# S5's inputs as products of x times the norm's weight, with the tokens' roots at the eviction, and S5's parameters on GpSimd

## The chip, the cores and the metric

One core of a Trainium2 chip runs the whole program in one launch. The metric is the device time in microseconds (us) of one execution. The engines are named as in the profile: PE (TensorE's matmuls; PEld its weight loads), DVE (VectorE), ACT (ScalarE), POOL (GpSimd) and SP (SyncE, which here only issues DMAs).

## What is computed

One layer of a decoder trunk over x (1024 tokens of 1024 channels, float32). Only the beginning matters here:

```python
h = x * rsqrt(mean(x * x, -1) + 1e-6) * norm_mix_pre
proj = h @ w_in          # columns: RWKV-7 parts | S5's input u (512) | two gates (2048)
# S5, 32 groups of 16 channels, 64 complex states each:
lam = a_re + 1j * a_im;  dt = exp(log_step);  a_bar = exp(lam * dt)
b_bar = ((a_bar - 1) / lam) * (b_re + 1j * b_im)
states = scan(a_bar, b_bar @ u);  y = Re(c @ states) + d * u
```

After it follow S5's GELU and gate, RWKV-7's recurrence, the merge of both branches, an output projection, and a gated MLP with a convolution, each with its norm.

## The kernel before

Everything is stored with channels on the 128 partitions and tokens along the free axis, in two halves of 512 tokens (`th` 0 and 1); x is 8 tiles of 128x512 per half. A float32 product is made of three matmuls on halves of the operands: `hi` is the operand rounded to fp32r (a cast on ACT), `lo` the rest (a subtraction on DVE or POOL), and hi*hi + hi*lo + lo*hi is accumulated (L169, L170, L171). So each 128x128 block of weights costs three matmuls of 128x512 per half.

The front of the program is this, in the order of PE's queue, which is that of the code (`manual_schedule` for PE; on the other engines the framework orders instructions by readiness and by the priorities HPN > HPW > HP2 > HP):

- Norm of half 0 (`norm`, L949 to L967): load x, square on ACT (L952), add pairs on DVE (L953), sum over channels by tiny matmuls against ones (`sumsq`, L242), the reciprocal root by bit trick and three Newton steps on DVE (`rstd` L262, `rsqrt` L131 to L136), its broadcast to all partitions by four transposes (`spread`, L268), a copy on ACT (`rbc`, L961). Then x times weight times root on DVE (L964) and its halves `hh` (ACT, L223) and `hl` (DVE or POOL, L224).
- S5's input u (`s5_in`, L1057): four output tiles (columns 14 to 17 of `w_in`), for both halves: 2 x 4 x 8 x 3 = 192 matmuls, in rounds of 12 for each of the 8 x tiles. Each of the four sums is copied out of PSUM by ACT (L1070) and written to DRAM (`US`), from where it comes back rearranged (`u8`).
- Norm of half 1, beside it, through the same steps.
- S5's parameters (`s5_setup`, L303 to L475): about 110 small operations on DVE, nearly all of 128x32, and a few sines on ACT.
- Then `mix_in` (L1034 on): the RWKV columns. Its first tile is column tile 12, which needs the scaled halves hh and hl of the norm. Beside it, S5's tables (`s5_tables`, L486 on) and scan run on DVE, and their small matmuls stand between those of `w_in`.

The parts after that are the same before and after the change.

Of the kernel before, what the change touches and what calls it, by code (L numbers as in the profile page):

```python
# [18 lines left out]
D = 1024  # L19
# [47 lines left out]
class Kern:  # L67
# [204 lines left out]
    def setup(self):  # L272
        nc = self.nc
        self.vecs = self.const.tile([128, NVEC], F32, name="vecs")
        self.csts = self.const.tile([128, NCST], F32, name="csts")
        nc.gpsimd.dma_start(self.csts[:, 0:128], self.a["cst"][:, 0:128])
        nc.gpsimd.dma_start(self.vecs, self.a["vec"])
        nc.gpsimd.dma_start(self.csts[:, 128:NCST], self.a["cst"][:, 128:NCST])
# [6 lines left out]

        o, n = VEC["mu"]
# [15 lines left out]
    def s5_setup(self):  # L302
        nc, V = self.nc, self.nc.vector  # L303
# [3 lines left out]
        with self.tc.tile_pool(name="s5tmp", bufs=1) as pool:  # L307
# [3 lines left out]
            nc.sync.dma_start(ls, a["s5_ls"])  # L311
            nc.sync.dma_start(lr, a["s5_a"][0])
            nc.sync.dma_start(li, a["s5_a"][1])
# [14 lines left out]
            def stt(x, sc, y, o0, o1):  # L328
                z = sm()
                V.scalar_tensor_tensor(z, x, sc, y, o0, o1)  # L330
                return z
# [50 lines left out]
            def sincos(x):  # L382
                x = ts(x, -PI_, PI_, ALU.max, ALU.min)
                si, co, ab = sm(), sm(), sm()
                nc.scalar.activation(si, x, AF.Sin)
# [17 lines left out]
            V.reciprocal(rd, d1)  # L403
# [71 lines left out]
            nc.sync.dma_start(s["d"], a["s5_d"])  # L475
# [460 lines left out]
    def load_x(self, th, pool):  # L936
        xs = []
        for k in range(NK):
            x = pool.tile([128, 512], F32, name=self.nm("x"), tag="x", bufs=16)
            self.nc.sync.dma_start(x, self.a["x"][k * 128:k * 128 + 128, th * 512:th * 512 + 512])  # L940
            xs.append(x)
        return xs

    def norm(self, th, xs, pool):

        nc = self.nc
        ss = self.chk()[:, 0:512]
        yield 0, T_X
        for k in range(0, NK, 2):  # L949
            sq = [pool.tile([128, 512], F32, tag="sq", name=self.nm("sq"), bufs=4) for _ in range(2)]  # L950
            for i in range(2):
                nc.scalar.activation(sq[i], xs[k + i], AF.Square)  # L952
            nc.vector.tensor_tensor(sq[0], sq[0], sq[1], ALU.add)  # L953
            self.sumsq(ss, sq[0], k == 0)
            yield 0.9, 1.0
        bc = self.chk()[:, 0:512]
        y = self.rstd(ss, 1e-6, 1.0 / D)
        yield 0, T_RS
        self.spread(bc, y)
# [97 lines left out]
    def s5_in(self, pool):  # L1057

        w = [self.load_w(self.a["w_in"][14 + b], pool=pool if b > 1 else None) for b in range(4)]
        for th in range(2):  # L1060
# [3 lines left out]
            for k in range(NK):  # L1064
                for b in range(4):
                    yield next(steps[b])
# [879 lines left out]
```

## Time and the profile before

| | us |
|---|---|
| median of 3 runs (lowest, highest) | 1556.08 (1554.93, 1562.61) |
| the profiled execution's own time | 1555.05 |
| its span in the profile | 1553.3 |
| PE busy in the span | 1455.0 |
| first matmul of S5's input | at 26.00 |
| first matmul of column tile 12, right behind S5's input | at 79.55 |

All times in the text are positions in the span or lengths, in us. In the lists of instructions, a row has its start, its length, the engine, the line in the kernel, the operation, output <- inputs, shapes, and in square brackets how long the engine was idle before it and what ended that. A length on DVE or POOL holds the time in which a started instruction could not get at its data; the start to start distance of neighbours shows the pipelined rate.

### The profile page before, as it was taken

To read this page: it belongs to the slowest core of one execution; us is meant where nothing else is said; L and a number is where in the kernel's file an instruction comes from. 1 tells how busy PE (TensorE), PEld (TensorE's weight loads), DVE (VectorE), ACT (ScalarE), POOL (GpSimd) and SP (SyncE) were. 2 spreads that over 40 slices of the span, in tenths; PEclk is the share of its full clock that TensorE was granted. 3 is DMA by queue.
4 is the path that set the end of the run, shared out by engine and by line. 5 is a ranking of instruction groups with operands and counts; after the bars stand their busy time and mean duration, and the time that the engine had idled before them with its cause. 6 is when DMAs were issued, how large, how long until landed. Compare 5 with 4: busy or idle time off the path is not lost. (4 is left out here: it accounts for less than half of the span.)

```text
span 1553.3 us, 24246 instructions
## 1 busy us (share of the span) xinstructions
PE 1455.0 (94%) x9324; PEld 1189.1 (77%) x9324; DVE 1092.0 (70%) x1777; ACT 682.4 (44%) x1061; POOL 135.9 (9%) x161
## 2 busy tenths in 40 slices
PE   5999899899999798999888999999999999999994
PEld 4787788778878586777776888788888887888783
DVE  6798784745326649547786689777777777697676
ACT  5354442433324444436434455444444444443450
POOL 2120000621103410100000000000000000000000
PEclk9999999999999999999998999999999999999997
DMA  6164342633413564524874444222222226934712
GB/s 208 41 202 119 93 126 92 203 116 109 152 48 99 158 193 145 148 70 111 263 232 154 160 146 142 82 87 84 85 88 84 82 69 230 325 129 148 240 60 94
DMA packets 131107, 210.45 MB, mean 135 GB/s; under 512 B 37696, under 2 KB 43840, under 8 KB 130992
## 3 DMA queue, kind: packets, MB, share of 16 engines
q1 hardware_dynamic: 124208, 188.32, 38.6%
q0 software_dynamic: 5632, 18.49, 3.7%
q10 hardware_dynamic: 1152, 2.10, 0.4%
q8 instruction: 73, 1.20, 0.3%
q14 instruction: 42, 0.34, 0.1%
HBM read 153.28 MB, written 53.48 MB: 133 GB/s over the span
## 5 line engine op out<-in xcount | busy, mean ns | idle before, releaser
L169 PE MATMUL gm<-hh,wh 128*128 128x512 f32 x688 | 283.0, 411 | 14.8 <-DVE hl L1115 8.9
L170 PE MATMUL gm<-hl,wh 128*128 128x512 f32 x688 | 271.4, 394 | 0.4 <-DVE hl L224 0.4
L171 PE MATMUL gm<-hh,wl 128*128 128x512 f32 x656 | 258.1, 394 | 0.0
L154 DVE TENSOR_TENSOR wl<-wf,wh 128x512 fp32r<-128x512 f32 x175 | 124.2, 711 | 116.0 <-ACT wh L153 106.9
L153 ACT CAST wh<-wf 128x512 fp32r<-128x512 f32 x179 | 110.5, 618 | 207.1 <-PE gm L170 118.5
L169 PEld LDWEIGHTS gm<-hh,wh 128*128 128x128 f32 x688 | 131.1, 190 | 50.1 <-DVE hl L1115 10.9
L170 PEld LDWEIGHTS gm<-hl,wh 128*128 128x128 f32 x688 | 131.0, 190 | 26.1 <-issue 1.0
L171 PEld LDWEIGHTS gm<-hh,wl 128*128 128x128 f32 x656 | 124.3, 190 | 27.3
L1554 PE MATMUL d<-xl,wh 128*128 128x512 f32 x308 | 121.7, 395 | 6.9 <-DVE xl L224 6.9
L1553 PE MATMUL d<-xh,wh 128*128 128x512 f32 x308 | 121.3, 394 | 2.1 <-ACT xh L223 2.1
L1555 PE MATMUL d<-xh,wl 128*128 128x512 f32 x308 | 120.9, 393 | 0.0
L1379 PE MATMUL rp<-t,h 128*128 128x512 f32 x216 | 84.4, 391 | 1.8 <-ACT p L1393 1.8
L1381 PE MATMUL rp<-t,l 128*128 128x512 f32 x216 | 84.1, 390 | 0.5 <-DVE l L224 0.5
L1380 PE MATMUL rp<-t,h 128*128 128x512 f32 x216 | 84.1, 389 | 0.0
L1554 PEld LDWEIGHTS d<-xl,wh 128*128 128x128 f32 x308 | 58.6, 190 | 20.7 <-DVE xl L224 8.6
L1553 PEld LDWEIGHTS d<-xh,wh 128*128 128x128 f32 x308 | 58.4, 190 | 14.7 <-ACT xh L223 2.5
L1555 PEld LDWEIGHTS d<-xh,wl 128*128 128x128 f32 x308 | 58.7, 191 | 12.3
L223 ACT CAST h<-r 128x1024 fp32r<-128x1024 f32 x34 | 35.8, 1054 | 61.1 <-PE rp L1380 29.6
L224 DVE TENSOR_TENSOR l<-r,h 128x1024 fp32r<-128x1024 f32 x34 | 41.6, 1225 | 29.2 <-ACT h L223 27.7
L1400 DVE SCALAR_TENSOR_TENSOR y<-zv,vecs,y 128x1023 f32<-128x1023 f32 (+1 forms) x36 | 46.1, 1281 | 8.6 <-ACT y L1398 8.6
L1379 PEld LDWEIGHTS rp<-t,h 128*128 128x128 f32 x216 | 40.5, 188 | 11.3 <-ACT p L1393 2.7
L1381 PEld LDWEIGHTS rp<-t,l 128*128 128x128 f32 x216 | 40.5, 188 | 9.4 <-DVE l L224 1.0
(451 smaller groups left out, 3244.0 us busy)
## 6 DMA issues: line engine op xcount, KB each, us to landing
r<-in_w_up_dram SPq DMA_DIRECT2D x36, 512.0 KB, 3.6
wf<-in_w_in_dram SPq DMA_DIRECT2D x68, 256.0 KB, 3.1
st<-in_w_down_dram SPq DMA_DIRECT2D x55, 256.0 KB, 4.2
st<-ACT SPq DMA_DIRECT2D x44, 256.0 KB, 4.5
wf<-in_w_up_dram SPq DMA_DIRECT2D x36, 256.0 KB, 2.8
ACT<-y POOLq DMA_DIRECT2D x18, 512.0 KB, 2.9
GT<-ev SPq DMA_DIRECT2D x32, 256.0 KB, 2.4
wf<-in_w_br_dram SPq DMA_DIRECT2D x32, 256.0 KB, 3.4
```

The lines of the kernel that those rows point to most:

```text
L153: nc.scalar.copy(h[:, :n], f[:, :n])
L154: nc.vector.tensor_tensor(l[:, :n], f[:, :n], h[:, :n].bitcast(F32), ALU.subtract)
L169: mm(ps, a, xh[k], start=k == 0, stop=False)
L170: mm(ps, a, xl[k], start=False, stop=False)
L171: mm(ps, b, xh[k], start=False, stop=k == n - 1)
L1379: mm(ps, wh[:, c], xh, start=first and k == 0, stop=False, skip_group_check=True)
L1380: mm(ps, wh[:, c], xl, start=False, stop=False, skip_group_check=True)
L1381: mm(ps, wl[:, c], xh, start=False, stop=k == 3, skip_group_check=True)
L1400: V.scalar_tensor_tensor(y[:, lag:], z[:, 0:1024 - lag], self.vec(nme, i), y[:, lag:], ALU.mult, ALU.add)
L1553: mm(ps, wh[:, c], xh[:, x], start=start, stop=False, skip_group_check=True)
L1554: mm(ps, wh[:, c], xl[:, x], start=False, stop=False, skip_group_check=True)
L1555: mm(ps, wl[:, c], xh[:, x], start=False, stop=stop, skip_group_check=True)
```

## The change

S5's input is no longer made from the finished norm. `start` loads x and the weights first of all, forms x times the norm's weight alone (`gained`: ACT's cast with a scale, DVE's rest with the same scale), multiplies that with the four weight tiles, and multiplies each token's root in when the sums leave PSUM (`evict`, on DVE in place of ACT's copy). The scaled halves that the other columns need (`scaled`) are made afterwards, into the same buffers, when S5's matmuls have read the unscaled ones. The squares are summed on DVE and POOL to one tile per half, so that four tiny matmuls per half are left of 16. The vectors of parameters come on ACT's DMA queue, the large constants on SP's behind x. The first weight tiles land in the `u8` buffers, which are free until then. `s5_setup` runs on POOL (only the reciprocal stays on DVE; a scalar_tensor_tensor becomes two POOL operations), its four small loads are on POOL's queue, and its sines are tied behind ACT's copy of the broadcast root of half 0.

```diff
--- before.py
+++ after.py
@@ -273,9 +273,8 @@
         nc = self.nc
         self.vecs = self.const.tile([128, NVEC], F32, name="vecs")
         self.csts = self.const.tile([128, NCST], F32, name="csts")
+        nc.scalar.dma_start(self.vecs, self.a["vec"])
         nc.gpsimd.dma_start(self.csts[:, 0:128], self.a["cst"][:, 0:128])
-        nc.gpsimd.dma_start(self.vecs, self.a["vec"])
-        nc.gpsimd.dma_start(self.csts[:, 128:NCST], self.a["cst"][:, 128:NCST])
         self.ones1 = self.const.tile([128, 1], F32, name="ones1")
         nc.gpsimd.memset(self.ones1, 1.0)
         self.last = self.const.tile([128, 14], F32, name="last")
@@ -283,6 +282,8 @@
         self.hpi = self.const.tile([128, 1], F32, name="hpi")
         nc.gpsimd.memset(self.hpi, math.pi / 2)

+    def setup_vecs(self):
+        nc = self.nc
         o, n = VEC["mu"]
         self.mu1 = self.const.tile([128, n], F32, name="mu1")
         nc.vector.tensor_scalar(self.mu1, self.vecs[:, o:o + n], -1.0, 1.0, ALU.mult, ALU.add)
@@ -300,7 +301,7 @@


     def s5_setup(self):
-        nc, V = self.nc, self.nc.vector
+        nc, V = self.nc, self.nc.gpsimd
         c = self.s5c
         a = self.a
         self.s5 = s = {}
@@ -308,9 +309,9 @@
             def sm(n=32, dt=F32):
                 return pool.tile([128, n], dt, name=self.nm("sm"))
             lr, li, ls = sm(), sm(), sm()
-            nc.sync.dma_start(ls, a["s5_ls"])
-            nc.sync.dma_start(lr, a["s5_a"][0])
-            nc.sync.dma_start(li, a["s5_a"][1])
+            nc.gpsimd.dma_start(ls, a["s5_ls"])
+            nc.gpsimd.dma_start(lr, a["s5_a"][0])
+            nc.gpsimd.dma_start(li, a["s5_a"][1])

             def ts(x, s1, s2, o0, o1=None, out=None, n=32):
                 y = out if out is not None else sm(n)
@@ -327,7 +328,8 @@

             def stt(x, sc, y, o0, o1):
                 z = sm()
-                V.scalar_tensor_tensor(z, x, sc, y, o0, o1)
+                V.tensor_scalar(z, x, sc, None, o0)
+                V.tensor_tensor(z, z, y, o1)
                 return z

             def rnd(x, sc):
@@ -382,6 +384,7 @@
             def sincos(x):
                 x = ts(x, -PI_, PI_, ALU.max, ALU.min)
                 si, co, ab = sm(), sm(), sm()
+                nc.scalar.copy(si[:, 0:1], self.rbc[:, 0:1])
                 nc.scalar.activation(si, x, AF.Sin)
                 nc.scalar.activation(ab, x, AF.Abs)
                 nc.scalar.activation(co, ab, AF.Sin, bias=self.hpi, scale=-1.0)
@@ -400,7 +403,7 @@
             d2 = tt(li, li, ALU.mult)
             d1 = tt(d1, d2, ALU.add)
             rd = sm()
-            V.reciprocal(rd, d1)
+            nc.vector.reciprocal(rd, d1)
             u1, u2 = tt(nr, lr, ALU.mult), tt(ni, li, ALU.mult)
             qr = tt(tt(u1, u2, ALU.add), rd, ALU.mult)
             u1, u2 = tt(ni, lr, ALU.mult), tt(nr, li, ALU.mult)
@@ -472,7 +475,7 @@
             V.tensor_scalar(q2[64:128], ar[64:128], -1.0, None, ALU.mult)
             s["q1"], s["q2"] = q1, q2
             s["d"] = c.tile([16, 32], F32, name="s5d")
-            nc.sync.dma_start(s["d"], a["s5_d"])
+            nc.gpsimd.dma_start(s["d"], a["s5_d"])


     def s5_load(self, b):
@@ -933,38 +936,121 @@
                 yield from self.mm3_steps(ps, w, 0, [h[0] for h in self.h[th]], [h[1] for h in self.h[th]])
                 use(th, ps)

-    def load_x(self, th, pool):
...
-    def norm(self, th, xs, pool):
...
+    def start(self, pool):
+
+        nc, V, A, G = self.nc, self.nc.vector, self.nc.scalar, self.nc.gpsimd
+        raw = {}
+        xs = [[pool.tile([128, 512], F32, name=self.nm("x"), tag="x", bufs=16) for k in range(NK)] for th in range(2)]
+        w = [([], []) for b in range(4)]
+
+        def load_x(th, k):
+            nc.sync.dma_start(xs[th][k], self.a["x"][k * 128:k * 128 + 128, th * 512:th * 512 + 512])
+
+        def load_w(b, i):
+            if b < 3:
+                f = self.u8[b].rearrange("p g n -> p (g n)")[:, i * 512:i * 512 + 512]
+            else:
+                f = self.wp.tile([128, 512], F32, tag="wf", name=self.nm("wf"), bufs=NWF)
+            raw[b, i] = f
+            nc.sync.dma_start(f, self.a["w_in"][14 + b][:, i * 512:i * 512 + 512])
+
+        def split_w(b, i):
+            own = pool if b > 1 else self.wp
+            h = own.tile([128, 512], F32R, tag="wh", name=self.nm("wh"), bufs=4 if b > 1 else NWH)
+            l = self.lx() if b > 1 else own.tile([128, 512], F32R, tag="wl", name=self.nm("wl"), bufs=NWL)
+            self.split(h, l, raw[b, i])
+            w[b][0].append(h)
+            w[b][1].append(l)
+
+        def gained(th, k):
+            hi, lo = self.pair(th, k)
+            g = self.vec("g_mix_pre", k)
+            A.activation(hi, xs[th][k], AF.Identity, scale=g)
+            V.scalar_tensor_tensor(lo, xs[th][k], g, hi.bitcast(F32), ALU.mult, ALU.subtract)
+            return hi, lo
+
+        def square(th, k):
+            sq = pool.tile([128, 512], F32, tag="sq", name=self.nm("sq"), bufs=4)
+            A.activation(sq, xs[th][k], AF.Square)
+            if k % 2:
+                (G if th or k < 4 else V).tensor_tensor(sq, sq, last[th], ALU.add)
+                if acc[th] is not None:
+                    V.tensor_tensor(sq, sq, acc[th], ALU.add)
+                acc[th] = sq
+            last[th] = sq
+
+        def root(th):
+            self.sumsq(sums[th][:, 0:512], acc[th], True)
+            return self.rstd(sums[th], 1e-6, 1.0 / D)
+
+        def scales(th, y):
+            bc = sums[th][:, 512:1024]
+            self.spread(bc, y)
+            r = pool.tile([128, 512], F32, tag="rbc", name=self.nm("rbc"), bufs=2)
+            A.copy(r, bc)
+            return r
+
+        def scaled(th, k):
+            x = xs[th][k]
+            V.scalar_tensor_tensor(x, x, self.vec("g_mix_pre", k), rbc[th], ALU.mult, ALU.mult)
+            self.h[th][k] = self.hsplit(x, k, self.hp[th], eng=G if k % 2 else V)
+
+        def evict(th, b, ps):
+            y = self.ev((128, 8, 64))
+            p, r = [x.rearrange("p (n j) -> p n j", j=8)[:, :, ::-1] for x in (ps, rbc[th])]
+            V.tensor_tensor(y.rearrange("p i n -> p n i"), p, r, ALU.mult)
+            nc.sync.dma_start(self.US[b].rearrange("i c g n -> (c g) i n")[:, :, th * 64:th * 64 + 64], y)
+            if self.stored is not None:
+                self.load_u8(self.stored)
+                self.stored = None
+            if th:
+                self.stored = b
+
+        load_x(0, 0)
+        for i in range(2):
+            for b in range(4):
+                load_w(b, i)
+            for k in range(4 * i, 4 * i + 4):
+                if k:
+                    load_x(0, k)
         for k in range(NK):
+            load_x(1, k)
+        nc.sync.dma_start(self.csts[:, 128:NCST], self.a["cst"][:, 128:NCST])
+        self.s5_load(0)
+        self.s5_load(1)
+        self.h = [[None] * NK, [None] * NK]
+        sums, last, acc, rbc = [self.chk() for th in range(2)], [None, None], [None, None], [None, None]
+        g = [[], []]
         for k in range(NK):
+            g[0].append(gained(0, k))
+            if k % 4 == 0:
+                for b in range(4):
+                    split_w(b, k // 4)
+            square(0, k)
+        for th in range(2):
+            ps = [self.gmp() for b in range(4)]
+            for k in range(NK):
+                for b in range(4):
+                    a, l = [x[k // 4][:, k % 4 * 128:k % 4 * 128 + 128] for x in w[b]]
+                    hi, lo = g[th][k]
+                    nc.tensor.matmul(ps[b], a, hi, start=k == 0, stop=False)
+                    nc.tensor.matmul(ps[b], a, lo, start=False, stop=False)
+                    nc.tensor.matmul(ps[b], l, hi, start=False, stop=k == NK - 1)
+                    if k == NK - 1:
+                        evict(th, b, ps[b])
+                if k == (1 if th else 4):
+                    y = root(th)
+                if k == (3 if th else 6):
+                    rbc[th] = scales(th, y)
+                    self.rbc = rbc[0]
+                if th:
+                    scaled(0, k)
+                elif k >= 4:
+                    for q in (2 * k - 8, 2 * k - 7):
+                        g[1].append(gained(1, q))
+                        square(1, q)
+        for k in range(NK):
+            scaled(1, k)

     def shifted(self, ps, mt, th):

@@ -1053,27 +1139,6 @@

         self.nc.sync.dma_start(self.u8[b], self.US[b].rearrange("i c g n -> (i c) g n"))
         self.s5_in_done = b
-
-    def s5_in(self, pool):
...

     def pair(self, where, k):

@@ -1757,21 +1822,15 @@
             self.u8 = [u8p.tile([128, 8, 128], F32, name=f"u8_{b}") for b in range(4)]
             with tc.tile_pool(name="xp", bufs=1) as xp:
                 with tc.high_priority(HPN):
-                    xs = [self.load_x(0, xp)]
                     self.setup()
                     self.s5w = {}
-                    self.s5_load(0)
-                    self.s5_load(1)
-                    for _ in self.norm(0, xs[0], xp):
-                        pass
-                    xs.append(self.load_x(1, xp))
-                self.fill = [self.s5_in(xp), self.mix_in()] + [self.gate_tiles(m) for m in range(14)] + [
+                    self.start(xp)
+                    self.setup_vecs()
+                with tc.high_priority(HP):
+                    self.s5_setup()
+                self.fill = [self.mix_in()] + [self.gate_tiles(m) for m in range(14)] + [
                     self.merge_loads(), self.gate_tiles(14, 15)]
                 self.outs, self.yr = 0, []
-                self.drive([(HPN, self.norm(1, xs[1], xp))])
-                self.drain(lambda: self.stored == 3)
-                with tc.high_priority(HP):
-                    self.s5_setup()
             with tc.tile_pool(name="s5p", bufs=1) as self.s5p:
                 self.s5d = [{} for _ in range(4)]
                 self.tabs = self.s5_done = -1
...
-T_X = 8.0
```

What this does to the queues is shown at three places, with the rows of each engine's list in order.

On POOL, the list before goes from the memsets at the start straight to the rests of the norm's halves (`hl`), of which these are the first five:

```order
L1688 MEMSET pad 128x8
L224 ISA
L224 TENSOR_TENSOR hl_307<-x_186,hh_306 128x512
L224 TENSOR_TENSOR hl_317<-x_190,hh_316 128x512
L224 TENSOR_TENSOR hl_327<-x_194,hh_326 128x512
L224 TENSOR_TENSOR hl_337<-x_198,hh_336 128x512
L224 TENSOR_TENSOR hl_552<-x_342,hh_551 128x512
```

In the list after, these rows stand on POOL ahead of the adds of half 1's squares (`sq_435` is the first, tiles x_202 and x_203); `sm` are 128x32 tiles of `s5_setup`, `s5rho` one of its results:

```order
L332 TENSOR_TENSOR sm_858<-sm_858,sm_838 128x32
L326 TENSOR_TENSOR sm_873<-sm_871,sm_858 128x32
L326 TENSOR_TENSOR sm_877<-sm_873,sm_875 128x32
L319 TENSOR_SCALAR sm_879<-sm_877 128x32
L326 TENSOR_TENSOR sm_1007<-sm_879 128x32
L326 TENSOR_TENSOR sm_1009<-sm_1007 128x32
L446 TENSOR_TENSOR s5rho<-sm_1009 128x32
L976 TENSOR_TENSOR sq_435<-sq_435,sq_429 128x512
L976 TENSOR_TENSOR sq_460<-sq_460,sq_454 128x512
L976 TENSOR_TENSOR sq_492<-sq_492,sq_486 128x512
L976 TENSOR_TENSOR sq_530<-sq_530,sq_524 128x512
```

From `s5_setup`'s first row to `s5rho` these are 97 rows: 95 small ones, of which 75 wait for an earlier row of POOL, and two adds of 128x512 (`sq_281` and `sq_294`, of half 0). Behind `sq_530` stand some fifty more rows of `s5_setup`, and only then the rests of the scaled halves.

On DVE, the root of half 0 before (`rv`, `rsy`, `rsh`) stands behind the adds of half 0 and between rests of weights, with nothing of half 1 ahead of it:

```order
L953 TENSOR_TENSOR sq_269<-sq_269,sq_270 128x512
L154 TENSOR_TENSOR lx_382<-wf_383,wh_381 128x512
L262 TENSOR_SCALAR rv_279<-chk_241 128x4
L154 TENSOR_TENSOR lx_388<-wf_389,wh_387 128x512
L131 TENSOR_SCALAR rsy_281<-rv_279 128x4
L132 TENSOR_SCALAR rsy_281<-rsy_281 128x4
L134 TENSOR_TENSOR rsh_282<-rsy_281 128x4
L135 SCALAR_TENSOR_TENSOR rsh_282<-rsh_282,rv_279 128x4
L136 SCALAR_TENSOR_TENSOR rsy_281<-rsh_282,rsy_281 128x4
```

After, the last two Newton steps of half 0's root (`rsy_412`) stand among work of half 1: the rests `hl` of its last three x tiles (x_207 to x_209), and the running sum of its squares, which takes what POOL's adds give:

```order
L134 TENSOR_TENSOR rsh_413<-rsy_412 128x4
L969 SCALAR_TENSOR_TENSOR hl_489<-x_207,vecs,hh_488 128x512
L135 SCALAR_TENSOR_TENSOR rsh_413<-rsh_413,rv_410 128x4
L136 SCALAR_TENSOR_TENSOR rsy_412<-rsh_413,rsy_412 128x4
L978 TENSOR_TENSOR sq_492<-sq_492,sq_460 128x512
L134 TENSOR_TENSOR rsh_413<-rsy_412 128x4
L969 SCALAR_TENSOR_TENSOR hl_521<-x_208,vecs,hh_520 128x512
L135 SCALAR_TENSOR_TENSOR rsh_413<-rsh_413,rv_410 128x4
L969 SCALAR_TENSOR_TENSOR hl_527<-x_209,vecs,hh_526 128x512
L136 SCALAR_TENSOR_TENSOR rsy_412<-rsh_413,rsy_412 128x4
L978 TENSOR_TENSOR sq_530<-sq_530,sq_492 128x512
L995 SCALAR_TENSOR_TENSOR x_194<-x_194,vecs,rbc_480 128x512
```

Three rows ahead of this piece stands the DVE add of `sq_460` and `sq_435`, both made by POOL.

On PE, the broadcast of that root (L268) stood before in front of all matmuls of S5's input. After, it stands between the seventh and the eighth round of half 0 (`gm_345` is the fourth sum's tile, `hh_328` and `hh_334` are x tiles 7 and 8):

```order
L1036 MATMUL gm_345<-hh_328,wh_314 128x512
L1037 MATMUL gm_345<-hl_329,wh_314 128x512
L1038 MATMUL gm_345<-hh_328,lx_315 128x512
L268 MATMUL chk_253<-csts,rsy_412 128x128 x4
L1036 MATMUL gm_342<-hh_334,wh_302 128x512
L1037 MATMUL gm_342<-hl_335,wh_302 128x512
```

44 lines of the change are left out of this document (removed).

## The prediction

> **What bounds the kernel now.** The page first.
>
> ```profile
> span 1553.3 us, 24246 instructions
> PE 1455.0 (94%) x9324; PEld 1189.1 (77%) x9324; DVE 1092.0 (70%) x1777; ACT 682.4 (44%) x1061; POOL 135.9 (9%) x161
> PE   5999899899999798999888999999999999999994
> ```
>
> PE bounds the span; its only poor slice is the first (38.8 us each). So the change is worth what it does to the time at which PE gets through the front. The windows view of that front, and who ended PE's waits:
>
> ```profile
> core 0: us, PE busy (x) PEld busy (x) DVE busy (x) ACT busy (x) POOL busy (x), PEclk, DMA share, GB/s
> 0.00:10.00 10.00, 0.00 (x0) 0.00 (x0) 1.76 (x9) 3.16 (x5) 2.29 (x12) 1.00 0.75 233
> 20.00:30.00 10.00, 4.69 (x12) 3.20 (x13) 8.44 (x21) 5.09 (x9) 1.67 (x1) 1.00 0.76 223
> 60.00:70.00 10.00, 10.00 (x45) 8.26 (x44) 9.87 (x33) 3.17 (x6) 2.98 (x2) 1.00 0.22 46
> 70.00:80.00 10.00, 10.00 (x46) 8.26 (x44) 1.57 (x3) 2.52 (x4) 0.41 (x1) 1.00 0.15 52
> ...
> PE chk L242 <- DVE sq L953: 12.8, 2, 11.5
> PE chk L268 <- DVE rsy L136: 2.9, 1, 2.9
> PE gm L169 <- ACT hh L223: 2.1, 1, 2.1
> ```
>
> PE waits for the norm, then hardly at all. The timeline has the ends of the stretch:
>
> ```profile
> 26.00 0.80 PE L169 MATMUL gm<-hh,wh 128*128 128x512 f32 x1 [2.11 <-ACT hh L223]
> 28.67 0.63 PE L170 MATMUL gm<-hl,wh 128*128 128x512 f32 x1
> 29.09 0.63 PE L171 MATMUL gm<-hh,wl 128*128 128x512 f32 x1
> 32.69 0.39 PE L169 MATMUL gm<-hh,wh 128*128 128x512 f32 x1
> 32.92 0.39 PE L170 MATMUL gm<-hl,wh 128*128 128x512 f32 x1
> 79.32 0.39 PE L171 MATMUL gm<-hh,lx 128*128 128x512 f32 x1
> 79.55 0.39 PE L169 MATMUL gm<-hh,wh 128*128 128x512 f32 x1
> ```
>
> S5's 192 matmuls begin at 26.00; tile 12, which needs scaled halves, at 79.55. A matmul costs 0.42 start to start at first and 0.23 once PE has run for about 5.7 us. **The sum is the shift of that 79.55**; behind it PE's list is the same work.
>
> **What the change removes.** The first matmul no longer waits for a root. ACT's list after starts with a table load (1.28) behind the first x tile, one scaled cast and one weight cast:
>
> ```profile
> 0.74 1.28 ACT L153 ACT_TABLE_LOAD   x1 [0.74 <-PEq L1934]
> 3.62 0.62 ACT L153 CAST wh<-wf 128x512 fp32r<-128x512 f32 x1 [1.60 <-DMA wf<-in_w_in_dram]
> 9.98 2.56 ACT L952 ACTIVATE sq<-x 128x512 f32<-128x512 f32 x4 [1.63 <-DMA x<-in_x_dram]
> ```
>
> The first tile of SP's queue landed at 3.62; 3.6 + 1.3 + 2 x 0.64 = 6.2. So PE starts 20 us earlier, and without a new wait this would be nearly the gain. I cost DVE's relief from `s5_setup` at nothing: DVE is busy 1.57 of the ten us before 79.55 already.
>
> **What it adds: POOL's chain.** The square of x's second tile is ACT's eighth row of 0.64, so done at 3.6 + 1.3 + 5.1 = 10.0; there POOL's 97 rows begin in earnest. What a small one costs, this trace shows only from afar:
>
> ```profile
> 288.58 1.21 POOL L667 TENSOR_SCALAR bk<-ld,ka_h,ka 128x512 f32<-128x512 f32 x1
> 289.87 1.60 POOL L668 TENSOR_TENSOR bk<-bk,ld 128x512 f32<-128x512 f32 x1
> ...
> L771 POOL MEMSET mt<- 128x32 f32 x2 | 0.5, 225 | 0.0
> L447 POOL MEMSET s5ar<- 128x32 f32 x1 | 0.1, 144 | 0.0
> L622 POOL MEMSET S<- 128x256 f32 x1 | 0.4, 414 | 0.0
> ```
>
> Memsets of the same 128x32 take 0.14 to 0.23, and a row that needs the one before starts 0.08 after its end (288.58 + 1.21 to 289.87); 75 of the 95 do. I take 0.18 + 0.08 = 0.26, with 0.14 (the shortest memset, no gap) and 0.41 (that of 128x256) as ends: 94 x 0.26 = 24.4, and two big adds of 1.3 (the row at 63.73 below).
>
> POOL is not alone, though. Here the timeline has DVE and POOL side by side:
>
> ```profile
> 33.01 0.74 DVE L964 SCALAR_TENSOR_TENSOR x<-x,vecs,rbc 128x512 f32<-128x512 f32 x1
> 37.45 1.61 POOL L224 TENSOR_TENSOR hl<-x,hh 128x512 fp32r<-128x512 f32 x1 [1.28 <-ACT hh L223]
> 37.85 1.26 DVE L320 TENSOR_SCALAR sm<-sm 128x32 f32<-128x32 f32 x1
> 54.71 0.68 DVE L224 TENSOR_TENSOR hl<-x,hh 128x512 fp32r<-128x512 f32 x1
> 54.86 1.67 POOL L224 TENSOR_TENSOR hl<-x,hh 128x512 fp32r<-128x512 f32 x1 [15.80 <-ACT hh L223]
> 55.31 1.77 DVE L964 SCALAR_TENSOR_TENSOR x<-x,vecs,rbc 128x512 f32<-128x512 f32 x1
> 63.73 1.30 POOL L224 TENSOR_TENSOR hl<-x,hh 128x512 fp32r<-128x512 f32 x1 [1.28 <-ACT hh L223]
> ```
>
> DVE's product of 0.74 takes 1.77 and ends 0.55 after POOL's add; a 128x32 operation takes 1.26, until POOL's 1.61 is over; POOL's 1.30 becomes 1.67 when DVE was at work as it began. They take turns. While DVE makes the rests of weights and x (19 operations of 0.65 up to its own wait on POOL), POOL gives a turn away before a row: I count 16 x 0.65 = 10.4, between 0 and 19 turns. So `sq_435` begins at **10.0 + 2.6 + 24.4 + 10.4 = 47.4**; DMA is not late by then (x's last tile is the 26th of 128x512 float32 on SP's queue, 6.8 MB: at the first window's 233 GB/s it is in by 32).
>
> The Trainium skill, "GPSIMD Engine Reference" (section 8), says that this engine shares its SBUF interfaces with VectorE and collides with instructions that have two SBUF inputs; the rows at 54.86 and 55.31 agree. By that rule the 10.4 stand; without turns the sum would end at 1562.
>
> **The wait that it makes.** From there to PE's broadcast (L268) everything is one chain: POOL's adds `sq_435`, `sq_460`, `sq_492` (3 x 1.3; ACT's squares have four buffers and wait for these adds), between them two ACT squares (1.3), then on DVE the running sum 0.7, two rests 1.4, three root steps 0.5, and two turns to POOL, 1.9: **10**. Behind DVE's waiting add stand half 0's last root steps, and behind those, in PE's queue, the eighth round of half 0 and all of half 1. PE has done its seven rounds by about 37 and stands still until 57.4.
>
> **From the broadcast to tile 12** there are two lists. PE: broadcast and round eight with short breath, 1.1 + 12 x 0.42 = 6.1; half 1, 96 x 0.23 = 21.8; sums and second broadcast 1.1; waits for the evictions about 1 and for the second root, which again stands behind ten products on DVE, about 3: 33. DVE and POOL, taking turns from the end of the evictions (6.9 behind the broadcast): 27 big DVE operations x 0.65 = 17.6, twelve root steps 2.2, 27 small POOL rows left x 0.3 = 8.1, and of POOL's eight rests at 1.2 between none and all: 34.8 to 44.4, at whose end stands the eviction for which tile 12's first matmul waits. I take 38, three rests. Tile 12 then starts at 47.4 + 10 + 38 = 95.4, **15.9 later** than at 79.55.
>
> **The tail.** The evictions of half 1 now stand on DVE in front of S5's tables:
>
> ```profile
> 79.42 2.99 ACT L1070 COPY ev<-gm 128x512 f32<-128x512 f32 x3
> 80.18 0.29 DVE L505 TENSOR_TENSOR sml<-s_b,s5q 128x128 f32<-128x128 f32 x1
> ...
> PE chk L611 <- DVE t L605: 4.3, 2, 2.4
> PE chk L541 <- DVE t L597: 1.8, 1, 1.8
> ```
>
> On ACT one took about 1.0; four of 0.7 to 1.0 put the tables about 3 us further behind tile 12. Their first product for PE has slack, the scan does not (1.8 of wait already): 0 to 3, I take 1.5. Sum: 15.9 + 1.5 = 17.4; 1555.05 + 17.4 = 1572.5. The execution lies 1.03 below the median of the runs, so against runs **1573**.
>
> On DVE the same parameter steps start 0.10 apart:
>
> ```profile
> 39.87 0.18 DVE L330 SCALAR_TENSOR_TENSOR sm<-sm,sm 128x32 f32<-128x32 f32 x1
> 39.97 0.17 DVE L318 TENSOR_SCALAR sm<-sm 128x32 f32<-128x32 f32 x1
> ```
>
> The Trainium skill, same page (section 3.1), has a two-input add on GpSimd at 1.96 times VectorE's time; by the page a row would be about 0.2 (an estimate), `sq_435` 5.6 earlier and the total 1567.
>
> **The rivals.**
> 1. *POOL is quick and PE is fed (faster).* Rows of 0.14, no turns: 10.0 + 2.6 + 13.2 = 25.8. The broadcast then waits for POOL and for the last x tile alike, at about 36; tile 12 follows 33 to 34 later, at 70: 9.5 gained, with a tail of 1 1546.5. For it: memsets at 0.14. Against: all these rows wait for each other and read two operands, and the turns are in the rows. Chance 0.15.
> 2. *It cancels out (no change).* Rows of 0.2 and few turns: 10.0 + 2.6 + 18.8 + 2.0 = 33.4, plus 10, plus 36: 79.4, so 1555 to 1558. The early start is then spent entirely on the wait in the middle. Chance 0.18.
> 3. *The forecast (slower).* Place: PE's broadcast of half 0 behind POOL's 97 rows. It decides as soon as `sq_435` starts later than about 34 (79.55 less 36 and 10). 1573, by itself 1564 to 1584. Chance 0.57.
> 4. *The same, with dear rows.* 0.41 each: 10.0 + 2.6 + 38.5 + 10.4 = 61.5, tile 12 at 109.5, 30 later: 1587. Chance 0.10.
>
> **How the numbers follow.** Likeliest 1573. The range leaves out rival 1 and the upper part of rival 4: 1552 to 1590. A measurement of this kernel tells about 0.5% (7.8 us) from no change; rival 1 is faster by just more than that, rival 2 within it, 3 and 4 slower: 0.15, 0.18, 0.67.
>
> **What the profile after would show.** Right: the first S5 matmul near 6; POOL busy from 10 to beyond 45 with small rows of 0.2 to 0.3, longer ones while DVE works; PE idle between about 37 and 57 in front of L268, the releaser named as DVE's root step; a second wait of some us before the second broadcast or tile 12; tile 12 near 95, and everything behind it shifted alike. Wrong: `s5rho` finished before 34 (then rival 1 or 2); POOL rows that cost the same beside DVE as alone (no turns); tile 12 late, but the end not (the later waits on S5's scan, 4.3 and 1.8 us, took it up); or PE's first rounds starved, with loads landing later than I have them.

## The result and the profile after

The changed kernel takes **1579.57 us** (median of 4 runs, 1575.54 to 1582.19) beside 1555.51 for the kernel before on the same chip (4 runs): a ratio of **1.0156**, 95% interval 1.0128 to 1.0184. The prediction was 1573, with a range of 1552 to 1590; the slowdown is 24 us by the medians, where 17.4 were forecast. The profiled execution took 1581.11, its span is 1579.3. Some executions fall into a slower state, and the ratios are taken without them, which leaves out one of experiment 8 (2411.84 us, at a granted clock of 0.555).

The page of the changed kernel: the span with its busy times, and the rows of the 40 slices (39.5 us each) for PE, POOL and PE's granted clock.

```profile
span 1579.3 us, 24219 instructions
PE 1456.7 (92%) x9276; PEld 1189.2 (75%) x9276; DVE 1100.4 (70%) x1677; ACT 684.3 (43%) x1071; POOL 196.8 (12%) x315
PE   6479989989999898899898999999999999999994
POOL 7842000351101421100000000000000000000000
PEclk9789999999999899999998999999999999999997
```

PE does the same work (1456.7 busy, 1455.0 before); what grew is its idle time, by 24 us. The second and third slices, which were 9 and 9, are 4 and 7. POOL, with little to do there before, is busy in the first three.

Who ended PE's waits in the first 150 us of the changed kernel (total, times, longest):

```profile
PE chk L268 <- DVE rsy L136: 24.1, 2, 22.9
PE gm L169 <- DVE ev L1001: 10.1, 1, 10.1
PE gm L1036 <- ACT wh L223: 6.8, 1, 6.8
PE chk L242 <- POOL sm L332: 3.0, 1, 3.0
```

The waits for the norm at the front (12.8, 2.9 and 2.1 us before) have become one of 6.8 for the first cast of weights. In its place stand 22.9 in front of the broadcast of half 0's root and 10.1 in front of tile 12. The chain that makes the 22.9, from the timelines of POOL, ACT, DVE and PE:

```profile
6.78 0.80 PE L1036 MATMUL gm<-hh,wh 128*128 128x512 f32 x1 [6.78 <-ACT wh L223]
47.70 0.24 POOL L446 TENSOR_TENSOR s5rho<-sm 128x32 f32<-128x32 f32 x1
47.89 1.26 POOL L976 TENSOR_TENSOR sq<-sq,sq 128x512 f32<-128x512 f32 x1
49.18 0.63 ACT L974 ACTIVATE sq<-x 128x512 f32<-128x512 f32 x1 [21.86 <-POOL sq L976]
51.19 0.69 DVE L978 TENSOR_TENSOR sq<-sq,sq 128x512 f32<-128x512 f32 x1 [21.85 <-POOL sq L976]
57.97 0.19 DVE L136 SCALAR_TENSOR_TENSOR rsy<-rsh,rsy 128x4 f32<-128x4 f32 x1
58.22 1.12 PE L268 MATMUL chk<-csts,rsy 128*128 128x128 f32 x4 [22.89 <-DVE rsy L136]
```

The last parameter row on POOL (`s5rho`), half 1's first add behind it, ACT's next square, which had waited 21.86 us for the buffer that this add frees, DVE's running sum, which had waited 21.85 for the second add, then the rest of the root, then PE. Behind it, the timelines at the second wait and at S5's first table product (L508, L505 before):

```profile
80.23 7.66 DVE L224 TENSOR_TENSOR hl<-x,hh 128x512 fp32r<-128x512 f32 x1
81.06 6.27 POOL L224 TENSOR_TENSOR hl<-x,hh 128x512 fp32r<-128x512 f32 x5
97.22 3.71 DVE L1001 TENSOR_TENSOR ev<-gm,rbc 128x512 f32<-128x512 f32 x4
98.38 0.77 PE L169 MATMUL gm<-hh,wh 128*128 128x512 f32 x1 [10.06 <-DVE ev L1001]
101.02 0.29 DVE L508 TENSOR_TENSOR sml<-s_b,s5q 128x128 f32<-128x128 f32 x1
101.93 0.63 PE L171 MATMUL gm<-hh,wl 128*128 128x512 f32 x1
```

One rest on DVE that takes 0.68 elsewhere took 7.66, as long as POOL made five rests without a break. Tile 12 begins at 98.38 instead of 79.55, the tables at 101.02 instead of 80.18. PE runs at about half its pace after its wait (0.43 from start to start, 0.23 later), so some 3 us later its list is 20.6 behind that of before (101.93, and 81.36 for the same matmul).

### The profile page after: what moved, and what is told of

Same layout as the page of the kernel before. It is cut to its first block, busy times and chain, and to the rows that moved or that the text cites. A ratio compares the mean times of both kernels' runs of the same rounds, so it can differ in the third digit from the quotient of the medians.

```text
span 1579.3 us, 24219 instructions
## 1 busy us (share of the span) xinstructions
PE 1456.7 (92%) x9276; PEld 1189.2 (75%) x9276; DVE 1100.4 (70%) x1677; ACT 684.3 (43%) x1071; POOL 196.8 (12%) x315
## 5 line engine op out<-in xcount | busy, mean ns | idle before, releaser
L169 PE MATMUL gm<-hh,wh 128*128 128x512 f32 x624 | 258.1, 414 | 22.2 <-DVE ev L1001 10.1
L170 PE MATMUL gm<-hl,wh 128*128 128x512 f32 x624 | 247.3, 396 | 0.0
L171 PE MATMUL gm<-hh,wl 128*128 128x512 f32 x624 | 246.8, 396 | 0.0
L153 ACT CAST wh<-wf 128x512 fp32r<-128x512 f32 x171 | 105.5, 619 | 186.3 <-PE gm L170 109.1
L169 PEld LDWEIGHTS gm<-hh,wh 128*128 128x128 f32 x624 | 119.4, 191 | 54.0 <-issue 13.2
L171 PEld LDWEIGHTS gm<-hh,wl 128*128 128x128 f32 x624 | 119.3, 191 | 26.2
L170 PEld LDWEIGHTS gm<-hl,wh 128*128 128x128 f32 x624 | 119.3, 191 | 23.6 <-issue 1.6
L1399 POOL DMA_DIRECT2D ACT<-y x18 | 9.6, 532 | 340.2 <-DVE y L1398 340.2
```

The costliest lines, as they stand in the source:

```text
L153: nc.scalar.copy(h[:, :n], f[:, :n])
L169: mm(ps, a, xh[k], start=k == 0, stop=False)
L170: mm(ps, a, xl[k], start=False, stop=False)
L171: mm(ps, b, xh[k], start=False, stop=k == n - 1)
```

## The experiments

The theory after the result: **whatever stands behind POOL's parameter rows in some queue is late**, first half 0's root. The rivals: the early start itself costs it (cold rounds, evictions with the root on DVE, later stages), or POOL's rests, which hold DVE up. Each ratio is against the kernel before on the same chip. All runs in one table, with the start of tile 12's first matmul and of the first table product in the profiled execution (10 is read from its trace alone):

| kernel | tile 12 | tables | ratio | 95% interval |
|---|---|---|---|---|
| before | 79.55 | 80.18 | 1 | |
| changed | 98.38 | 101.02 | 1.0156 | 1.0128 to 1.0184 |
| 1 parameters on DVE | 77.67 | 87.17 | 1.0060 | 1.0038 to 1.0083 |
| 2 adds on DVE | 76.01 | 87.67 | 1.0082 | 1.0067 to 1.0098 |
| 3 rests on DVE | 93.79 | 98.23 | 1.0116 | 1.0092 to 1.0139 |
| 4 before, parameters on POOL | 110.15 | 110.79 | 1.0232 | 1.0199 to 1.0264 |
| 5 adds and rests on DVE | 78.72 | 83.17 | 1.0022 | 1.0000 to 1.0045 |
| 6 as 1, plain evictions | 72.76 | 82.54 | 1.0012 | 0.9993 to 1.0030 |
| 7 as 1, only half 0 early | 77.83 | 78.75 | 0.9999 | 0.9981 to 1.0016 |
| 8 as 7, parameters on POOL | 85.51 | 86.14 | 1.0045 | 1.0022 to 1.0067 |
| 9 as 8, sines tied back | 69.82 | 75.34 | 0.9983 | 0.9966 to 0.9999 |
| 11 changed, plain evictions | 89.99 | 97.11 | 1.0133 | 1.0107 to 1.0159 |
| 12 before, longer tables | 79.36 | 79.99 | 1.0036 | 1.0016 to 1.0056 |

**1. The parameters back on DVE.**

```diff
 def s5_setup(self):
-    nc, V = self.nc, self.nc.gpsimd
+    nc, V = self.nc, self.nc.vector
...
-    V.tensor_scalar(z, x, sc, None, o0)
-    V.tensor_tensor(z, z, y, o1)
+    V.scalar_tensor_tensor(z, x, sc, y, o0, o1)
```

> The changed kernel with S5's parameter steps back on DVE (with the joined two-step operations), all else as changed. Theory (half 0's root waits for half 1's square adds, which stand behind 97 parameter rows on POOL): the adds run as their squares come, PE's long wait before the broadcast L268 falls from 24 us to under 8, the broadcast comes at 37 to 43 instead of 58, tile 12 at 78 to 85 instead of 98.4, the time 1558 to 1566. Rival A (the early start itself, the evictions on DVE or the later stages cost it): the time stays above 1572. Rival B (it is POOL's rests that hold DVE up): the wait of 10 us before tile 12 stays and the time is 1568 to 1572.

Tile 12 came at 77.67, 20.7 earlier than in the changed kernel, and the broadcast at 40.22: the rows on POOL were the cause of the wait. The time of 1559.38 us is in the range expected (ratio 1.0060). But tile 12 is here 1.9 *ahead* of the kernel before, and the time is not. Two rows of its trace say where that went. PE's one wait from 80 to 150 us:

```profile
PE chk L552 <- DVE ca L532: 7.7, 1, 7.7
```

and the first table product, 7 us later than in the kernel before:

```profile
87.17 0.27 DVE L507 TENSOR_TENSOR sml<-s_b,s5q 128x128 f32<-128x128 f32 x1
```

**2. The adds of squares on DVE; 3. the rests on DVE; 4. one part alone, the parameters on POOL in the kernel before.**

```diff
 2
-    (G if th or k < 4 else V).tensor_tensor(sq, sq, last[th], ALU.add)
+    V.tensor_tensor(sq, sq, last[th], ALU.add)
 3
-    self.h[th][k] = self.hsplit(x, k, self.hp[th], eng=G if k % 2 else V)
+    self.h[th][k] = self.hsplit(x, k, self.hp[th], eng=V)
 4 (the kernel before, with the joined operation as two)
-    nc, V = self.nc, self.nc.vector
+    nc, V = self.nc, self.nc.gpsimd
```

> The changed kernel with every add of squares on DVE; the parameter steps stay on POOL. Theory: the 97 rows then stand ahead of nothing that PE waits for in half 0; DVE has six more adds of 0.7; the broadcast comes at 37 to 43, tile 12 at 80 to 88, the time 1560 to 1568. If POOL's rows cost by holding DVE up at the shared port, and not by the wait: the broadcast after 48 and the time above 1572. If the early start itself or the later stages cost it: above 1572 with the broadcast near 40.

> The changed kernel with all rests of the scaled halves on DVE, so that POOL makes none of them; all else as changed. Theory (two separate losses: the wait for the root, 24 us, and DVE's stand of 7.7 us behind POOL's five rests): the broadcast stays at 58, no DVE rest takes over 2 us, DVE has eight rests of 0.7 more, so tile 12 comes between 94 and 100 and the time is 1574 to 1582, that of the changed kernel within 0.4%. Rival B (the rests on POOL are the main cost): 1558 to 1568. Rival A: as the changed kernel, and no row moves at tile 12.

> The kernel before with one part of the change alone: S5's parameter steps on POOL, everything else as before. Here ACT's copy of half 1's root stands behind sines that wait for POOL's rows, and POOL's four rests of half 1 stand behind about 145 rows that start near 32 to 38. Theory (a row costs 0.3 to 0.6 us on POOL, and whatever stands behind the rows waits): the first of these rests begins at 85 to 100 instead of 54.9, the time is 1580 to 1600. Rival A (the parameter steps on POOL are harmless, the early start costs it): 1552 to 1560.

Experiment 2: the broadcast came at 32.40 and tile 12 at 76.01, both earlier than expected. The time of 1563.95 us is in the range expected, but with a tile 12 ahead of that of the kernel before, the theory leaves no reason for its being 0.82% longer. The timeline of POOL and DVE shows the next thing that stood behind POOL's rows:

```profile
77.68 9.95 POOL L224 TENSOR_TENSOR hl<-x,hh 128x512 fp32r<-128x512 f32 x8
87.67 0.29 DVE L508 TENSOR_TENSOR sml<-s_b,s5q 128x128 f32<-128x128 f32 x1 [9.12 <-POOL hl L224]
```

All eight rests that POOL makes came at the end of its rows, and the first table product, which by the order of the tile pools in the code takes over memory that the x tiles held, waits for the last of them. DVE stood 9.12 us. ACT's queue shows one thing more that was already behind these rows here:

```profile
41.63 0.23 ACT L389 ACTIVATE sm<-sm 128x32 f32<-128x32 f32 x1 [12.06 <-POOL sm L321]
44.97 0.56 ACT L990 COPY rbc<-chk 128x512 f32<-128x512 f32 x1
```

An absolute value of a parameter waited 12.06 us for a row of POOL. The copy of half 0's root stood behind it, until 44.97 although the broadcast came at 32.40, and PE waited 9.4 us for the first eviction, which needs that copy.

Experiment 3: a wait of 22.5 in front of the broadcast, as in the changed kernel, and tile 12 4.6 earlier than there (93.79, just ahead of the 94 to 100 expected). The time of 1570.82 us is below the 1574 to 1582 expected, on a chip where the kernel before takes 1551.44. The ratio of 1.0116 is below the changed kernel's 1.0156, but the intervals overlap. That POOL's rests are a second, smaller loss is shown by 2 and 5, which differ by them alone: 1.0082 and 1.0022, the intervals apart.

Experiment 4: here the rows stand ahead of POOL's four rests of half 1, and of sines and absolute values, for the first of which ACT's queue stood 20.63 us, with the copy of half 1's root behind it. POOL's timeline has the rests:

```profile
88.04 4.96 POOL L224 TENSOR_TENSOR hl<-x,hh 128x512 fp32r<-128x512 f32 x4
```

and the two longest of PE's waits from 26 to 130 us are

```profile
PE gm L170 <- POOL hl L224: 16.0, 1, 16.0
PE gm L169 <- ACT ev L1071: 12.4, 1, 12.4
```

The first of these rests ran at 88.04 (54.86 before), the time is 2.32% longer. **Moved alone, the parameters cost more than the whole change**, in which they begin near 10 us and not at 35.57 as here, and PE has a start of 19 us.

**5. Adds and rests on DVE; 6. as 1, with the evictions as plain copies.** In 6 the roots are left out of S5's input.

```diff
 5: the edits of 2 and 3 together
 6: the edit of 1, and
-    V.tensor_tensor(y.rearrange("p i n -> p n i"), p, r, ALU.mult)
+    A.copy(y.rearrange("p i n -> p n i"), p)
```

> The changed kernel with all adds of squares and all rests of the scaled halves on DVE; POOL keeps the parameter steps alone. In the run with only the adds moved, tile 12 began at 76.0, 3.5 us before that of the kernel before, and yet the time was 0.8% longer: S5's first table product stood until 87.7, where POOL's last rest of half 1 ended. Theory (what costs is everything that stands behind POOL's parameter rows, rests too): the first table product now starts at 78 to 84, and the ratio to the kernel before is 0.999 to 1.004. Rival (DVE's own added work, 16 rests of x times the weight and 8 evictions, and here 8 more rests, is the bound): the tables start at 86 or later, DVE without a gap ahead of them, ratio 1.006 or more.

> The first experiment (parameter steps back on DVE) with S5's evictions as plain copies on ACT: the roots are not multiplied in, so S5's input is left unscaled; all else as there. In that experiment tile 12 began at 77.7, and the time was still 0.6% above the kernel before, with DVE busy without a break and PE waiting 7.7 us for a table product near 107. Theory (DVE's added work is the second loss): eight evictions of about 1 us leave DVE, the wait of 7.7 falls below 3, the ratio falls to 0.998 to 1.003. Rival (that loss lies in the tables' loads or in later stages): the wait and the ratio of 1.006 stay.

Both as the theory had it. In 5 POOL keeps its rows, and no add and no rest stands behind them: the tables start at 83.17 and the loss is down from 1.56% to 0.22%. ACT's queue still stands behind them, as in 2 (an absolute value waits 12.11 us for a row of POOL), and PE waits 12.2 us for the first eviction, so what the rows cost by themselves is not shown by 5. In 6 the wait of 7.7 is 0.8:

```profile
PE chk L552 <- DVE ca L532: 0.8, 1, 0.8
```

and the ratio falls by 0.48 points, so eight evictions of about 1 us on DVE, with their wait for the root, cost about 7 us of time where DVE is busy up to the tables.

**7. Only half 0 early; 8. the same with the parameters on POOL; 9. with ACT's sines tied back.** Half 1's S5 input is made from its scaled halves as before the change, with plain evictions; half 0's scaled halves follow those of half 1, by a second copy of its root.

```diff
 7: the edit of 1, and
-    g[1].append(gained(1, q))
...
+    if th == 0:
+        rbc[1] = scales(1, root(1))
+        for k in range(NK):
+            scaled(1, k)
+        g[1] = self.h[1]
+        rbc[0] = pool.tile([128, 512], F32, tag="rbe", name=self.nm("rbe"), bufs=1)
+        A.copy(rbc[0][:, 0:1], rbc[1][:, 0:1])
+        A.copy(rbc[0], sums[0][:, 512:1024])
 8: this without the edit of 1, with those of 2 and 3
 9: as 8, and ahead of the absolute values and of the half angle's sine
+    nc.scalar.copy(ab[:, 0:1], self.rbc[:, 0:1])
+    nc.scalar.copy(sh[:, 0:1], self.rbc[:, 0:1])
```

> The first experiment (parameter steps on DVE) with only half 0 started early: half 1's S5 input is made from its scaled halves as in the kernel before, with plain evictions on ACT, and half 0's scaled halves follow behind those of half 1. DVE loses 8 rests and 4 evictions, about 10 us, against the first experiment. If DVE's sum up to the tables is the bound: the wait of 7.7 us for the table product goes or falls below 2, the ratio to the kernel before is 0.994 to 1.002. If it is not: ratio 1.004 or more.

> As the kernel with only half 0 early, but the parameter steps on POOL, where they stand ahead of nothing else: adds of squares and rests are on DVE. DVE then loses the parameter rows too, about 19 us, and gets 16 adds and rests, about 9 us. Theory (each of the two losses, work behind POOL's rows and work on DVE ahead of the tables, is taken away): tile 12 begins at 62 to 70, S5's tables at 72 to 80, the ratio is 0.990 to 0.999. If POOL's rows reach the tables late: tables after 82 and a ratio of 1.000 to 1.006. If PE's new waits between half 0 and half 1 eat it: a wait of over 8 us ahead of half 1's first round and tile 12 after 75.

> The kernel with only half 0 early and the parameter steps on POOL, with one thing more: all of ACT's sines and absolute values of the parameters now come behind the copy of half 0's root, where some had stood 17.7 us in ACT's queue waiting for a row of POOL, ahead of half 1's squares. Theory (whatever stands behind POOL's rows is late, ACT's queue too): half 0's broadcast comes at 34 to 39 instead of 47.9, S5's tables at 73 to 78 instead of 86.1, and the ratio to the kernel before is 0.993 to 1.000. If POOL's rows behind the sines are then too late for the tables: tables after 80 and a ratio over 1.000.

7 is level with the kernel before (0.9999): up to 130 us PE no longer waits for a table. 8 missed: I expected 0.990 to 0.999 and got 1.0045. I had moved everything from behind POOL's rows but ACT's queue. ACT's timeline:

```profile
37.31 0.23 ACT L389 ACTIVATE sm<-sm 128x32 f32<-128x32 f32 x1 [17.66 <-POOL sm L321]
```

It is the wait of 2 and 5 again: an absolute value of a parameter waited 17.66 us for a row of POOL, here with half 1's squares behind it; the broadcast of half 0 came at 47.89. With those functions tied behind the copy of half 0's root (9), it came at 29.56, sooner than the 34 to 39 expected, the tables start at 75.34, and the kernel takes 1550.06 us beside 1553.02: a ratio of **0.9983 (0.9966 to 0.9999)**. It is the one version of those tried that beats both kernels, the one before by some 3 us. The interval's upper end lies only just below 1, so this gain is weakly shown. Its tables wait for POOL's rows in the end:

```profile
75.34 0.29 DVE L510 TENSOR_TENSOR sml<-s_b,s5q 128x128 f32<-128x128 f32 x1 [4.79 <-POOL s5ai L469]
```

ACT's queue is not free of the rows here either:

```profile
40.16 0.23 ACT L389 ACTIVATE sm<-sm 128x32 f32<-128x32 f32 x1 [7.62 <-POOL sm L321]
43.41 0.59 ACT L992 COPY rbc<-chk 128x512 f32<-128x512 f32 x1
```

This time the copy of half 1's root stands behind the wait, though its broadcast came at 37.05, and PE waits 7.3 us in front of half 1's first round. No run tells what this costs at the end.

**10. The port by itself.** The changed kernel with eight adds on POOL and eight on DVE at the very start.

```diff
+    p = pool.tile([128, 512], F32, name=self.nm("sq"), tag="sq", bufs=4)
+    V.memset(p, 1.0)
+    t = [self.pair(1, k) for k in range(NK)]
+    for a, b in t:
+        G.tensor_tensor(a, p, p, ALU.add)
+        V.tensor_tensor(b, p, p, ALU.add)
     load_x(0, 0)
```

> The changed kernel with 16 adds more at its very start, when nothing else runs: eight on POOL and eight on DVE, 128x512 each, two SBUF operands, none waiting for another; their results are written over later. Alone such an add takes 1.26 us on POOL and 0.69 on DVE in this kernel's traces. If the two take turns (as I reckoned in the prediction): DVE's eight take 1.8 to 2.0 each, and both engines need 15 to 16 us. If the engine that has the port keeps it as long as its next add is ready (the theory for the rest of 7.66 us on DVE beside POOL's five): one of them runs its eight at its own pace and the other stands for all that time: DVE's eight begin 10 us late or POOL's 5.5 us late. If they do not disturb each other: 5.5 and 10 us side by side.

The view of these two lines (shortest, median and longest duration in ns, first and last start in us):

```profile
L1014 DVE TENSOR_TENSOR hl<-sq x8: 678/679/9222, 1.4 to 15.3; 128x512 fp32r<-128x512 f32 x8
L1013 POOL TENSOR_TENSOR hh<-sq x8: 1029/1030/1053, 2.7 to 9.7; 128x512 fp32r<-128x512 f32 x8
```

POOL's eight ran at 1.03 each without a pause. DVE's second add, at 2.0, lasted until 11.2, **9.22 us**, and the others went through behind it. No turns: DVE stood until POOL's eight adds were over.

**11. The changed kernel with plain evictions; 12. the kernel before with longer tables.** 11 has the eviction's edit of 6 alone and also leaves the roots out; 12:

```diff
-    for t, x, p in ((w, bw, s["ar"]), (wt, bx, s["ai"])):
+    for t, x, p in ([] if b else 8 * [(w, bw, s["ar"])]) + [(w, bw, s["ar"]), (wt, bx, s["ai"])]:
```

> The changed kernel with S5's evictions as plain copies on ACT: the roots are not multiplied in, so S5's input is left unscaled; all else as changed. It prices the tail (evictions on DVE ahead of S5's tables), which the prediction put at 1.5 us. Theory after the experiments so far (evictions of half 1 stand at the end of DVE's list, and tile 12 and the tables behind them): the broadcast stays at 58, tile 12 begins at 89 to 95 instead of 98.4, the tables at 95 to 99 instead of 101.0, the time falls by 3 to 8 us, ratio 1.010 to 1.014. If the evictions are hidden, as 1.5 us would have it: ratio 1.014 to 1.017.

> The kernel before with one thing added: the first product of S5's first table is written nine times instead of once, eight of 1.2 us more, so that DVE is about 9.4 us longer at the tables of batch 0; PE's way up to tile 12 is untouched. Over the runs so far the time goes with the start of the tables (16.9 us late with 1.33% in one, 4.8 us early with -0.17% in another) and not with the start of tile 12 (6.8 us early with +0.12%). Theory (DVE at the tables is what the end hangs on): 6 to 11 us longer, ratio 1.004 to 1.007, PE waiting for a table near 105 to 115. Rival (the tables have slack and the link is only chance, tile 12 counts): ratio 0.999 to 1.002.

11: tile 12 at 89.99, tables at 97.11 and a ratio of 1.0133, all within what was expected; but the interval overlaps that of the changed kernel, so the price of the evictions is shown by 6 and not by this. The locked port is there again, with DVE's rows beside POOL's runs of three and five rests:

```profile
79.95 5.16 DVE L995 SCALAR_TENSOR_TENSOR x<-x,vecs,rbc 128x512 f32<-128x512 f32 x1
89.57 7.61 DVE L154 TENSOR_TENSOR wl<-wf,wh 128x512 fp32r<-128x512 f32 x2
...
80.78 3.77 POOL L224 TENSOR_TENSOR hl<-x,hh 128x512 fp32r<-128x512 f32 x3
89.76 6.27 POOL L224 TENSOR_TENSOR hl<-x,hh 128x512 fp32r<-128x512 f32 x5
```

12: tile 12 is where it was, and PE waits 7.5 us for a table:

```profile
PE chk L541 <- DVE t L520: 7.5, 1, 7.5
```

The ratio, 1.0036, lies between the two ranges. Of about 9.4 us more on DVE, 5.4 arrive at the end. So the tables do bound the end by themselves, but not one for one: by its rows PE's list is 9.9 us late behind that wait and 6.2 from 150 us on, part of it a wait of 1.5 for an eviction that is gone.

## Why the prediction was right, and where its sizes were off

- **The first matmul** was put at 6.2; it ran at 6.78, after a wait for the cast named.
- **POOL's chain** was to bring half 1's first add at 47.4; it came at 47.89. The parts were less exact than the sum. The windows view of the changed kernel, alone and beside a busy DVE (the column of POOL stands behind ACT's):

```profile
17.50:27.30 9.80, 6.76 (x31) 5.46 (x29) 9.58 (x15) 7.28 (x12) 8.54 (x16) 0.88 0.53 157
29.00:47.70 18.70, 6.33 (x22) 4.75 (x20) 0.31 (x2) 0.00 (x0) 15.60 (x63) 0.68 0.12 34
```

  63 rows in 18.70 us are 0.30 each (0.26 assumed), 16 rows in 9.80 are 0.61 beside DVE (0.91 assumed, with a turn each). One row ran alone at 7.26; the first add, with which the rows begin in earnest, came at 10.47 (10.0 in the prediction). From there to 47.89, less the two adds, 34.8 us went into the small rows. At 0.30 each, 94 of them are about 28 (24.4 in the prediction), so about 7 came from DVE's work beside them (10.4 in the prediction); both are estimates from these rows. That too little and too much nearly cancelled is luck.
- **The wait that it makes**: the broadcast was put at 57.4, and came at 58.22; PE had been idle since 35.3 (37 in the prediction). Experiment 1 shows that the rows are its cause: the same kernel without them on POOL has the broadcast at 40.22. The wait grows through two links, ACT's buffers and the place of DVE's running sum ahead of the root steps, both named.
- **From the broadcast to tile 12** I took 38, with three of POOL's rests on the path; 40.2 were measured, so tile 12 began at 98.38 instead of 95.4. The term is inside its bounds (34.8 to 44.4), and the prediction had one mechanism in it wrong: it let DVE and POOL **take turns**. Experiment 10 shows that they don't once POOL has several independent operations ready, and the row of 7.66 is that case. The turns that I had seen were with POOL's rests one at a time, 1.28 us apart. The Trainium skill, "SBUF — State Buffer" (section "Who interferes with whom"), says that the shared port pair is locked for a whole instruction and the later one blocks; the row of 9.22 agrees with the lock, and goes further, since DVE stood for all eight instructions of POOL and not for one. Which of the two comes first is not settled by it: by the recorded starts DVE's row did (2.0, and 2.7 for POOL's first).
- **"The sum is the shift of that 79.55"** is the step that failed, though the total came out within 0.5%. In the changed kernel itself it can't be seen, since tile 12 and the tables are late there by nearly the same (18.8 and 20.8 us). The variants show it: in experiments 1, 2, 5 and 6 tile 12 begins 0.8 to 6.8 us before that of the kernel before, and none of them is faster. In the table the ratio goes with the start of S5's tables instead, from 75.34 with 0.9983 to 110.79 with 1.0232 (3 and 11 stand the other way round, and 12 has longer tables with an unchanged start). PE's list agrees: compared row by row with that of the kernel before, it is at 160 us 5.7 us late in 1, 6.5 late in 2 and 5.5 early in 9, near their tables (7.0 and 7.5 late, 4.8 early) and far from their tile 12 (1.9, 3.5 and 9.7 early). Experiment 12 delays the tables alone and lengthens the kernel. Here are DVE's row with the gap ahead of the tables in the kernel before, and the windows view of 1 from 64.5 us to its tables (the third pair is DVE):

```profile
78.14 0.69 DVE L154 TENSOR_TENSOR wl<-wf,wh 128x512 fp32r<-128x512 f32 x1 [7.69 <-PE gm L170]
...
64.50:87.17 22.67, 21.87 (x89) 17.59 (x88) 22.47 (x65) 8.46 (x16) 7.22 (x5) 0.92 0.38 97
```

  DVE was idle 7.69 us there before, and in 1 it is busy 22.47 of the 22.67 us. I read the gap as room that is worth nothing; it is the room that the tables have, and with the parameters on DVE the change fills it with 16 rests of x times the weight and eight evictions.
- **The tail** was put at 1.5, for tables behind the evictions. Of the 24.1 us by the medians, 18.8 are tile 12's shift. By its rows PE waits for no table up to 150 us in the changed kernel, so the tail is not a wait for tables there: the first 1.7 us are PE's half pace behind its wait, PE's list is some 20 us late between 200 and 280 us, and about 4 more come behind that. I could not place these: the profiled executions of the other versions gain or lose up to 5 us in the later stages. The mean granted clock was 0.961 against 0.976, but that difference lies in the front (0.84 against 1.00 in the first 130 us, 0.97 in both behind it). The 4 us stay open.
- **The rivals.** "POOL is quick" failed by the rows of 0.30, "it cancels out" by `sq_435` at 47.89 where 34 was the point that decides, "dear rows" by 0.30 instead of 0.41. None had a second bound behind PE's waits, which is what the variants without the long wait ran into.

## What to carry to other kernels

Before work is moved to an engine because that engine is idle, go through every queue in which something will then stand behind it: here the same rows held up adds, rests, a table that reuses memory and, by way of sines and absolute values, ACT's squares and copies of roots, and each showed only when the one before it was freed. Then ask which engine bounds the *next* stage: 9.4 us more on DVE at the tables cost 5.4 with PE's path untouched, and of 19 us gained at PE's first matmul the best version kept 3. By these runs, two engines that share a port can be planned as taking turns only where the slower one gets its operations singly.

## What the runs showed of the hardware

- POOL's independent two-input adds from SBUF, queued one behind the other, kept DVE's two-input instructions out for the whole run: 9.22 us beside eight of 1.03, 7.66 and 5.16 beside runs of five and three. A chain of small rows on POOL, most of them waiting for an earlier one, did not: there DVE got through, and the rows took 0.61 instead of 0.30.
- A 128x512 add on POOL took 1.03 us in experiment 10, with the same tile as both operands, and 1.26 in the changed kernel's row at 47.89 with two different ones.
